# MLP products in another order: product 2 of group 0 ahead of product 1 of group 1, and three changes near the stage's ends

## The chip, the core and the metric

The kernel runs on one core of one Trainium2 chip. The metric is the device time of one execution in microseconds (us). TensorE (PE) multiplies; VectorE (DVE), ScalarE (ACT) and GpSimd (POOL) prepare its operands and take its results out of PSUM; SyncE (SP) issues most DMA transfers. In the traces each engine's instructions follow one another in the order of its own list, and they wait on semaphores for the other engines.

## The reference, cut to what matters

```python
def squared_relu_mlp(h, w1, w2):
    u = jax.nn.relu(h @ w1)
    return (u * u) @ w2

# for each of the 2 layers, x of 512 x 1024, all in float32:
#   x = x + mixer(rms_norm(x, norm_mix[layer]))     layer 0: attention, layer 1: a gated recurrence
#   x = x + squared_relu_mlp(rms_norm(x, norm_mlp[layer]), mlp_w1[layer], mlp_w2[layer])   # 1024 -> 4096 -> 1024
# return rms_norm(x, norm_final)
```

The change lies in the two MLPs and in the last normalization.

## The kernel before, in words

Every float32 product is made of three matmuls in a reduced format: each operand is split into a high half (a copy in that format, made on ACT) and a low half (the difference, made on DVE), and high by high, high by low and low by high are added up in PSUM. In the traces the halves of weights are called `wh` and `wl`; those of the hidden activations are `bh` and `bl` for group 0 and `sh` and `sl` for group 1.

The hidden width of 4096 is worked off in four quarters, `q4` = 0 to 3. A quarter has an up stage (activations times `w1`, squared ReLU into the tiles `u`) and a down stage (`u` times `w2`, added to the tokens' result `c`). Both use a Strassen-Winograd scheme: seven products P1 to P7 of sums of quarter blocks in place of eight. In the down stage each product is done for two groups, `g` = 0 and 1, one after the other into the same pair of PSUM banks, and 12 matmuls of 128x512 make one product of one group. The scheme has three running sums, each with its own two banks: X (`ps_t` in the down stage; P1, P6, P7 and P4 add to it in turn), V (`ps_acc`; P5 and P3) and W (`ps_z`; P2). After a product's group 1 the running sum is read by `collect`, which scales it and adds it to a part of `c` (`c<-ps_t,rr,c`, two DVE instructions, one for each bank). The next product of the same sum adds into the very banks that `collect` reads, so its first matmul waits for that read.

The order of a down stage's products stands in the table `ORDERS`: "mid" for all quarters but the last one of layer 1, which has "last". The list `steps` is run through once. Ahead of step `i` the loop calls `leave(i - 1)`, which first collects what step `i - 1` finished, if its group was 1, and then calls `prepare(i + 3)`: it makes the operand of the product three steps on. Operands come from the weight blocks b11, b12, b21 and b22. `added` sums two blocks in place for P5 and P6 (on DVE, `b<-b,b`; for P7, P4 and the first P6 by a DMA that accumulates, issued by POOL); `make` then splits the sum, `wh` on ACT and `wl` on DVE. What `prepare` also does, at places 20, 22 and 23 of the 28 places of a quarter, is to split one more piece of group 1's activations (`split_slot`, `sl<-u,sh`). Order on DVE and on ACT within the MLP is fixed: the class `Ordered` chains each instruction to the one recorded before it. So the order of calls in `leave` is the order in which DVE works.

In quarter 0, at places 19, 20, 24 and 25, `leave` also makes sums of blocks of the input `x` for the up stages (`sums_of_x`) and their halves (`halves_of_sums`, with the tiles `low`).

In layer 1 `end` takes over the last two steps, P4 of both groups: bank 0 of X holds tokens' part (2,0) and bank 1 part (3,0). It collects them, squares and sums the finished rows on ACT, takes the root, scales with `both`, `one` and `scaled`, and stores; all stores are issued by SP.

Of the kernel before, what the change touches and what calls it, by code (L numbers as in the profile page):

```python
# [18 lines left out]
S = 512  # L19
# [42 lines left out]
def hybrid_encoder(  # L62
# [23 lines left out]
    nc = tc.nc  # L86
    V, A, G, PE = nc.vector, nc.scalar, nc.gpsimd, nc.tensor
# [122 lines left out]
    behind = [None]  # L210
# [89 lines left out]
    with ExitStack() as actx:  # L300
# [12 lines left out]
        for i in range(2):  # L313
            both = []
# [460 lines left out]
    class Mlp:  # L775
# [299 lines left out]
        def collect(self, name, i, ps, cols=slice(0, S)):  # L1075
# [9 lines left out]


        ORDERS = {
            "mid": "P1 0 P5 0 P1 1 P2 0 P5 1 P6 0 P6 1 P3 0 P3 1 P7 0 P7 1 P2 1 P4 0 P4 1",
            "last": "P1 0 P5 0 P1 1 P2 0 P5 1 P2 1 P6 0 P6 1 P3 0 P3 1 P7 0 P7 1 P4 0 P4 1",
        }  # L1090

        def order(self, kind):
# [24 lines left out]
        def run(self, first, between, end):  # L1117
# [13 lines left out]
            def place(i):  # L1131

                return (i + self.STEPS // 2) % self.STEPS
# [21 lines left out]
            def make(i):  # L1155
                if i >= len(steps):
                    return
                name = steps[i][3]
                kind, q4, p, name = steps[i]
                at = 0  # L1160
                if kind == "up":
                    at = self.OPEN_AT if (p, name) == (0, "P1") else UP_AT
                ws[i] = made[i] = self.operand(self.source(unit(i), name), at)

                for before, x in (("P5", "P7"), ("P6", "P4")):
                    if name == before:
                        self.added(unit(i), x)

            def prepare(i):

                if i < len(steps) and steps[i][0] == "up":

                    if steps[i][3] == "P7" or self.layer and steps[i][1:] == (1, 0, "P4"):
                        return
                if i - 1 in range(len(steps)) and i - 1 not in made and i > 2:
                    make(i - 1)
                if i < len(steps) and steps[i][0] == "down":
                    add(i, 0)
                    if waiting and place(i) in (20, 22, 23):
                        self.split_slot(*waiting.pop(0))  # L1180
                make(i)
                for n in range(i + 1, i + 6):
                    add(n, n - i)

# [23 lines left out]
                elif at == 25 and q4 < NQ - 1:  # L1208
                    self.load(units["up", q4 + 1], (1, "b12"), (1, "b22"))

            def prepare_or_hold(i):

                if i + 1 < len(steps) and steps[i + 1][0] == "up" and steps[i + 1][3] == "P1":
                    held.append(i + 4)
                else:
                    prepare(i + 4)

            def leave(i):

                if i < 0:  # L1220
                    return
                kind, q4, p, name = steps[i]
                bank = sums[kind, q4, p if kind == "up" else 0][self.PRODUCTS[name][3]]
                if kind == "down":
                    if p:
                        for n in range(2):
                            self.collect(name, n, bank[n])
                    prepare_or_hold(i)
                    if q4 == 0:

                        k = {19: 2, 20: 2, 24: 3, 25: 3}.get(place(i))
                        if k:
                            (self.sums_of_x if place(i) in (19, 24) else self.halves_of_sums)(k)
                        if place(i) == 26:
                            self.replace()
                    return
                u, three = us[p], bank.rearrange("p (i n) -> p i n", i=2)
                keep = {"P1": 0, "P6": 1, "P5": 2, "P7": 3}.get(name)
                if keep is not None:

                    self.A.copy(u[keep], three)
                if held:
                    prepare(held.pop())
                    if p:
                        self.sums(0, slice(0, 2), slice(1, 4))
                at, x, y, op = {
                    "P3": (1, three, u[1], ALU.subtract),
                    "P7": (2, u[2], u[3], ALU.subtract),
                    "P2": (0, u[0], three, ALU.add),
                    "P4": (3, three, None, None),  # L1250
                }.get(name, (None,) * 4)
                if op:
                    self.V.tensor_tensor(u[at], x, y, op)
                if name == "P4":
                    self.A.activation(u[3], three, AF.Relu)
                    self.square(u[3])
                    if p:
                        last_sums(u, self.SUMS[:2])
                if later:
                    later.pop()()  # L1260
                prepare_or_hold(i)
                if op:
                    def rest(u=u, at=at):
                        self.A.activation(u[at], u[at], AF.Relu)
                        self.square(u[at])
                        if p:
                            self.split_slot(p, u[at], at)

                    if p and name == "P3":
                        later.append(rest)  # L1270
                    else:
                        rest()
                    if name == "P2" and not p:
                        self.split(p, slice(0, 2), slice(0, 3), slice(0, 3))
                elif name == "P4" and p:
                    last_sums(u, self.SUMS[2:3])
                    self.split_slot(p, u[2], 5)
                    last_sums(u, self.SUMS[3:])
                    waiting[:] = [(p, u[j], 3 + j) for j in (0, 1, 3)]
                elif name == "P4":  # L1280
                    self.sums(p, slice(0, 2), slice(1))
                elif name in ("P5", "P6") and p:
                    n = ("P5", "P6").index(name)
                    self.split(0, n, slice(0, 4), slice(3, 7))
# [63 lines left out]
    with ExitStack() as mctx:  # L1348
        mlp = Mlp(mctx, 0)
# [4 lines left out]
        last = {}  # L1354
# [57 lines left out]
    with ExitStack() as rctx:  # L1412
# [90 lines left out]
        def scaled(c):  # L1503
            OV.tensor_tensor(ps[f"c{c}"], ps[f"c{c}"], r, ALU.mult)
# [114 lines left out]
    with ExitStack() as mctx:  # L1619
# [57 lines left out]
            V.reciprocal(rt, rt)  # L1677
            return rt

        def store(t, h, cols=slice(0, S)):  # L1680
            nc.sync.dma_start(
                out=out[t * P : (t + 1) * P, h * S + cols.start : h * S + cols.stop],
                in_=mlp.y(t, h)[:, cols],
            )

        def both(t, h, rt, cols=slice(0, S), last=None):

            y = mlp.y(t, h)[:, cols]
            with tc.issue_after(last.ins) if last else nullcontext():
                V.scalar_tensor_tensor(y, y, rt, gb[h][:, cols], ALU.mult, ALU.mult)  # L1690
            store(t, h, cols)

        def one(t, h, rt, cols=slice(0, S), e=A, last=None):

            y = mlp.y(t, h)[:, cols]
            if e is A:
                with tc.issue_after(last.ins) if last else nullcontext():
                    A.activation(y, y, AF.Copy, scale=rt)
            else:
                V.tensor_scalar(y, y, rt, None, ALU.mult)  # L1700
            store(t, h, cols)

        def end(ws, xs):
            EG.turn(True)
            for t in range(2):
                square(t, 0, 0)
                scaled(t, 0)
                square(t, 1, 1, end=True)
                rt = root(t, 1)
                one(t, 0, rt)  # L1710
                both(t, 1, rt, last=mlp.gained)
            square(2, 1, 0)
            scaled(2, 1)
            square(3, 1, 0)
            scaled(3, 1, behind=mlp.y(1, 1))
            for g in range(2):
                mlp.times("P4", g, 0, ws[g], xs[0], False)
            mlp.collect("P4", 0, xs[0])
            square(2, 0, 1, end=True)
            two = root(2, 1)  # L1720
            mlp.collect("P4", 1, xs[1])
            parts = [slice(i * HS, (i + 1) * HS) for i in range(2)]
            for i, cols in enumerate(parts):
                ps = mlp.bank()[:, :HS]
                for g in range(2):
                    mlp.times("P4", g, 1, ws[g], ps, True, cols)
                mlp.collect("P4", 1, ps, cols)
                sq = square(3, 0, 1 + i, cols, end=i == 1)
                if i == 0:
                    both(2, 0, two)  # L1730
                    one(2, 1, two, last=sq)
                    scaled(3, 0, cols, behind=mlp.y(2, 0))
            rt = root(3, 2)
            both(3, 0, rt, parts[1])
            one(3, 1, rt)
            one(3, 0, rt, parts[0], V)

        end.ready = factors
# [70 lines left out]
```

## Time and profile before

| | us |
|---|---|
| median of 3 runs (1030.96 to 1031.72) | 1031.44 |
| the profiled execution | 1031.54 |
| its span, first to last instruction | 1029.5 |
| TensorE busy in the span | 1018.6 |
| VectorE busy | 857.8 |
| ScalarE busy | 700.9 |
| GpSimd busy | 172.6 |
| mean granted TensorE clock | 0.998 |

The profile of one execution gives each instruction's start and length, and for idle time the instruction whose end released it. `L765` is the helper of `Ordered`, so nearly all DVE and ACT instructions of the MLPs stand under that one line and are told apart by their tiles. The down stages' matmuls are line 1107, the up stages' 976, the last P4's 1070. A row that ends in x2 merges two instructions that follow each other.

### The profile page before, as it was taken

The page shows a single profiled execution, that of the slowest core. Times are in us where ns is not written, and L with a number is a line of the kernel's source. Part 1 is how long each engine was busy: PE and PEld are TensorE (multiplying, and loading weights), DVE is VectorE, ACT ScalarE, POOL GpSimd, SP SyncE. Part 2 cuts the span into 40 slices and gives each one's busy share as a digit, 9 for nine tenths or more (in the row PEclk, how much of TensorE's full clock was granted, in tenths as well). Part 3 has the DMA queues.
Part 4 walks back from the last instruction along what each step waited for, and adds up shares of the span by engine and source line. Part 5 has one row for each costly group of instructions (what it writes and reads, how often), then busy time and mean ns, then how long its engine had stood idle before and what let it go on. Part 6 is the DMA issues. An engine that isn't in the chain of part 4 may idle for free.

```text
span 1029.5 us, 15878 instructions
## 1 busy us (share of the span) xinstructions
PE 1018.6 (99%) x5862; PEld 892.2 (87%) x5862; DVE 857.8 (83%) x1148; ACT 700.9 (68%) x1083; POOL 172.6 (17%) x239
## 2 busy tenths in 40 slices
PE   8999999999999999999999999999999999999997
PEld 7888888888888988988988888888888988988986
DVE  6888787847789798898899888984689898898897
ACT  6777676835766873873875799964755774874865
POOL 0344344420010010010011121200010010010013
PEclk9999999999999999999999999999999999999999
DMA  7745454537537677667683575452436777677653
GB/s 236 216 124 144 105 153 103 155 110 265 156 81 197 169 156 194 174 146 199 177 209 80 156 184 151 103 220 86 97 71 182 169 159 196 168 149 200 174 109 111
DMA packets 53260, 160.46 MB, mean 156 GB/s; under 512 B 6720, under 2 KB 8256, under 8 KB 53184
## 3 DMA queue, kind: packets, MB, share of 16 engines
q1 hardware_dynamic: 42096, 120.35, 35.7%
q0 software_dynamic: 10656, 38.80, 23.1%
q8 instruction: 46, 0.75, 0.3%
q10 hardware_dynamic: 432, 0.31, 0.1%
q14 instruction: 30, 0.25, 0.1%
HBM read 137.41 MB, written 4.19 MB: 138 GB/s over the span
## 4 chain that ended last, share of the span: by engine, by line
PE 87%; DVE 6%; ACT 3%; issue 2%; DMA 1%; POOL 0%; SPq 0%; DVEq 0%; ACTq 0%; POOLq 0%
PE ps_t L1107 13%; PE ps_acc L1107 8%; PE ps_acc L976 7%; PE ps_z L976 5%; PE ps_acc L229 5%; PE ps_acc L231 5%; PE ps_acc L230 5%; PE ps_z L1107 4%; PE ps_o L976 3%; DVE wl L765 2%; PE ps_t L229 2%; PE ps_t L231 2%; PE ps_t L230 2%; PE ps_o L229 2%; PE ps_o L231 2%; PE ps_o L230 2%
## 5 line engine op out<-in xcount | busy, mean ns | idle before, releaser
L765 ACT CAST wh<-b 128x1024 fp32r<-128x1024 f32 x168 | 173.9, 1050 | 118.5 <-DVE b L765 73.5
L765 DVE TENSOR_TENSOR wl<-b,wh 128x1024 fp32r<-128x1024 f32 x168 | 202.9, 1219 | 38.9 <-ACT wh L765 37.6
L1052 POOL DMA_DIRECT2D b<-in_w_dn x40 | 35.0, 874 | 363.9 <-DVE b L765 268.4
L229 PE MATMUL ps_acc<-xgh,wh 128*128 128x512 f32 x192 | 78.5, 409 | 0.0
L231 PE MATMUL ps_acc<-xgl,wh 128*128 128x512 f32 x192 | 75.2, 392 | 0.0
L230 PE MATMUL ps_acc<-xgh,wl 128*128 128x512 f32 x192 | 75.1, 391 | 0.0
L224 DVE TENSOR_TENSOR wl<-raw,wh 128x512 fp32r<-128x512 f32 (+2 forms) x70 | 61.9, 912 | 14.2 <-ACT wh L222 14.1
L589 DVE TENSOR_TENSOR_SCAN scan<-keep,later 128x128 f32<-128x128 f32 (+1 forms) x64 | 59.5, 934 | 17.0 <-ACT keep L579 11.6
L765 ACT ACTIVATE u<-u 128x512 f32<-128x512 f32 x100 | 63.1, 633 | 11.3 <-DVE u L765 9.7
L222 ACT CAST wh<-raw 128x512 fp32r<-128x512 f32 (+2 forms) x70 | 50.6, 758 | 20.9 <-PE ps_acc L231 7.3
L593 POOL TENSOR_TENSOR w<-w,scan 128x128 f32<-128x128 f32 (+1 forms) x64 | 51.7, 809 | 57.2 <-DVE scan L589 54.0
L765 DVE TENSOR_TENSOR b<-b,b 128x1024 f32<-128x1024 f32 x48 | 58.7, 1223 | 1.3
L1052 POOL DMA_DIRECT2D b<-in_w_up x24 | 20.8, 868 | 231.1 <-DVE b L765 67.0
L765 DVE TENSOR_TENSOR u<-u 128x512 f32<-128x512 f32 (+1 forms) x92 | 54.9, 596 | 4.1 <-ACT u L765 2.1
L765 ACT CAST wh<-raw 128x1024 fp32r<-128x1024 f32 x46 | 48.1, 1047 | 2.5 <-PE ps_acc L1107 2.4
L1107 PE MATMUL ps_t<-wh,sl 128*128 128x512 f32 x120 | 47.0, 391 | 0.4 <-DVE sl L765 0.2
L1107 PE MATMUL ps_t<-wh,bh 128*128 128x512 f32 x120 | 46.8, 390 | 0.0
L1107 PE MATMUL ps_t<-wh,bl 128*128 128x512 f32 x120 | 46.8, 390 | 0.0
L1107 PE MATMUL ps_t<-wh,sh 128*128 128x512 f32 x120 | 46.7, 390 | 0.0
L765 DVE TENSOR_TENSOR sl<-u,sh 128x512 fp32r<-128x512 f32 (+2 forms) x50 | 37.4, 749 | 10.3 <-ACT sh L765 10.3
L976 PE MATMUL ps_acc<-low,wh 128*128 128x256 f32 x192 | 44.9, 277 | 0.5 <-DVE low L765 0.5
L765 DVE TENSOR_TENSOR wl<-raw,wh 128x1024 fp32r<-128x1024 f32 x36 | 44.3, 1229 | 0.8 <-ACT wh L765 0.8
(411 smaller groups left out, 3211.7 us busy)
## 6 DMA issues: line engine op xcount, KB each, us to landing
b<-in_w_dn SPq DMA_DIRECT2D x48, 512.0 KB, 4.4
b<-in_w_dn POOLq DMA_DIRECT2D x40, 512.0 KB, 5.8
b<-in_w_up SPq DMA_DIRECT2D x36, 512.0 KB, 4.8
b<-in_w_up POOLq DMA_DIRECT2D x24, 512.0 KB, 5.6
raw<-in_w_m SPq DMA_DIRECT2D x16, 512.0 KB, 4.5
raw<-in_w_dn SPq DMA_DIRECT2D x16, 512.0 KB, 4.6
raw<-in_w_in SPq DMA_DIRECT2D x16, 512.0 KB, 4.1
raw<-in_w_qk SPq DMA_DIRECT2D x12, 512.0 KB, 3.6
```

The costliest lines, as they stand in the source:

```text
L222: A.copy(wh[:, k, :], raw[:, k, :])
L224: V.tensor_tensor(wl[:, k, :], raw[:, k, :], f(wh[:, k, :]), ALU.subtract)
L229: PE.matmul(ps, wh, ah, start=start, stop=False)
L230: PE.matmul(ps, wl, ah, start=False, stop=False)
L231: PE.matmul(ps, wh, al, start=False, stop=stop)
L589: V.tensor_tensor_scan(sc[:, S - n : S][:, ::-1], keep[:, :n][:, ::-1], later[:, S - n :][:, ::-1], 1.0, ALU.mult, ALU.max,)
L593: G.tensor_tensor(wt, wt, sc[:, S - n + 1 : S + 1], ALU.mult)
L765: ins = getattr(self.e, name)(*args, **kwargs)
L976: PE.matmul(ps[:, i * HS : (i + 1) * HS], m, y, start=new and i == k == low == 0 and y is h, stop=(low, i, k) == steps[-1], skip_group_che ...
L1052: G.dma_start(out=unit[b].rearrange("p j n -> p (j n)"), in_=unit["src"](to), accum_op=ALU.add)
L1107: PE.matmul(sums[to][i], m, y[:, j, :], start=new and g == j == low == 0 and m is h, stop=g == low == j == 1, skip_group_check=not new,)
```

## The change

The order of products in a down stage is changed: P2 of group 0 is step 2 and P1 of group 1 is step 3, the other way round than before. In quarter 0, at place 25, the low halves of x's sums are made directly behind the operand, ahead of the additions of weights that `prepare` records last. In the end of layer 1 the running sum X is collected once more before P4, which then has a bank of its own for part (2,0) and is collected from it a second time; `both(2, 0)` moves behind the last half's collect; the store of part (3,1) is issued by ACT.

```diff
         ORDERS = {
-            "mid": "P1 0 P5 0 P1 1 P2 0 P5 1 P6 0 P6 1 P3 0 P3 1 P7 0 P7 1 P2 1 P4 0 P4 1",
-            "last": "P1 0 P5 0 P1 1 P2 0 P5 1 P2 1 P6 0 P6 1 P3 0 P3 1 P7 0 P7 1 P4 0 P4 1",
+            "mid": "P1 0 P5 0 P2 0 P1 1 P5 1 P6 0 P6 1 P3 0 P3 1 P7 0 P7 1 P2 1 P4 0 P4 1",
+            "last": "P1 0 P5 0 P2 0 P1 1 P5 1 P2 1 P6 0 P6 1 P3 0 P3 1 P7 0 P7 1 P4 0 P4 1",
         }
...
+            def prepare(i, then=None):
...
                 make(i)
+                if then:
+                    then()
                 for n in range(i + 1, i + 6):
                     add(n, n - i)
...
-                    prepare_or_hold(i)
+                    k = {19: 2, 20: 2, 24: 3, 25: 3}.get(place(i)) if q4 == 0 else None
+                    sums_or_halves = self.sums_of_x if place(i) in (19, 24) else self.halves_of_sums
+                    ahead = place(i) == 25 and k
+                    prepare_or_hold(i, (lambda: sums_or_halves(k)) if ahead else None)
                     if q4 == 0:
-                        k = {19: 2, 20: 2, 24: 3, 25: 3}.get(place(i))
-                        if k:
-                            (self.sums_of_x if place(i) in (19, 24) else self.halves_of_sums)(k)
+                        if k and not ahead:
+                            sums_or_halves(k)
...
         def end(ws, xs):
...
+            for i in range(2):
+                mlp.collect("P4", i, xs[i])
+            ps = mlp.bank()
             for g in range(2):
-                mlp.times("P4", g, 0, ws[g], xs[0], False)
-            mlp.collect("P4", 0, xs[0])
+                mlp.times("P4", g, 0, ws[g], ps, True)
+            mlp.collect("P4", 0, ps)
             square(2, 0, 1, end=True)
             two = root(2, 1)
-            mlp.collect("P4", 1, xs[1])
...
                 if i == 0:
-                    both(2, 0, two)
                     one(2, 1, two, last=sq)
-                    scaled(3, 0, cols, behind=mlp.y(2, 0))
+                    scaled(3, 0, cols, behind=mlp.y(3, 0)[:, cols])
+                else:
+                    both(2, 0, two, last=mlp.gained)
             rt = root(3, 2)
             both(3, 0, rt, parts[1])
-            one(3, 1, rt)
+            one(3, 1, rt, queue=A)
```

On DVE, at the start of quarter 2's down stage in layer 0, the instructions change places as follows (a minus is before, a plus is now). `wl<-raw` is the low half of P2's operand, `wl<-b_4740` that of P1 of group 1, `b_4740<-b_4740,b_4976` the addition for P5 of group 1, and `sl` and `u` are group 1's activations.

```order
 L765 TENSOR_TENSOR sl<-u,sh 128x2x256
 L765 TENSOR_TENSOR u<-u,ps_o 128x512
+L765 TENSOR_TENSOR wl<-raw,wh 128x1024
+L765 TENSOR_TENSOR sl<-u,sh 128x2x256
+L765 TENSOR_TENSOR u<-u 128x512 x2
 L765 TENSOR_TENSOR wl<-b_4740,wh 128x1024
 L765 TENSOR_TENSOR b_4740<-b_4740,b_4976 128x1024
-L765 TENSOR_TENSOR sl<-u,sh 128x2x256
-L765 TENSOR_TENSOR u<-u 128x512 x2
-L765 TENSOR_TENSOR wl<-raw,wh 128x1024
 L765 TENSOR_TENSOR u<-u 128x512
 L765 TENSOR_TENSOR sl<-u,sh 128x2x256
```

The low half of P1's operand and the addition behind it have moved behind the activations' instructions.

Some instructions further on DVE does the following. The first two rows are the low halves of P5 of group 1 and P6 of group 0; `b_4740<-b_4740,b_4980` is the addition for P6 of group 1, the third `wl` is the low half of that sum; `c_3131<-ps_t` is the collect of P1, `wl<-b_4978` the operand of P3, `c_3134<-ps_acc` the collect of P5.

```order
 L765 TENSOR_TENSOR wl<-b_4740,wh 128x1024
 L765 TENSOR_TENSOR wl<-b_4736,wh 128x1024
+L765 TENSOR_TENSOR b_4740<-b_4740,b_4980 128x1024
+L765 TENSOR_TENSOR sl<-u,sh 128x2x256
+L765 TENSOR_TENSOR wl<-b_4740,wh 128x1024
 L765 SCALAR_TENSOR_TENSOR c_3131<-ps_t,rr,c_3131 128x512 x2
-L765 TENSOR_TENSOR b_4740<-b_4740,b_4980 128x1024
-L765 TENSOR_TENSOR sl<-u,sh 128x2x256
-L765 TENSOR_TENSOR wl<-b_4740,wh 128x1024
 L765 TENSOR_TENSOR wl<-b_4978,wh 128x1024
 L765 SCALAR_TENSOR_TENSOR c_3134<-ps_acc,rr,c_3134 128x512 x2
```

The collect of P1 now stands behind the three instructions that make P6's operand of group 1; before, it stood ahead of them.

On DVE in quarter 0 of layer 1, near the end of the down stage, the three `low` rows are the low halves of x's sums and `b_7954<-b_7954,b_7958` is an addition of weights for the next up stage.

```order
 L765 SCALAR_TENSOR_TENSOR c_7345<-ps_z,rr,c_7345 128x512 x2
 L765 TENSOR_TENSOR wl<-b_7954,wh 128x1024
-L765 TENSOR_TENSOR b_7954<-b_7954,b_7958 128x1024
 L765 TENSOR_TENSOR low<-x,bl 128x256
 L765 TENSOR_TENSOR low<-x,s_7933 128x256
 L765 TENSOR_TENSOR low<-x,s_7352 128x512
+L765 TENSOR_TENSOR b_7954<-b_7954,b_7958 128x1024
 L765 TENSOR_TENSOR wl<-b_7954,wh 128x1024
 L765 SCALAR_TENSOR_TENSOR c_7347<-ps_t,rr,c_7347 128x512 x2
```

The addition has moved behind the three low halves.

## The prediction and its working

> **What bounds the kernel now.** I read the page first: how busy each engine is, and the clock.
>
> ```profile
> span 1029.5 us, 15878 instructions
> PE 1018.6 (99%) x5862; PEld 892.2 (87%) x5862; DVE 857.8 (83%) x1148; ACT 700.9 (68%) x1083; POOL 172.6 (17%) x239
> PEclk9999999999999999999999999999999999999999
> ```
>
> TensorE is busy for 1018.6 of 1029.5 us at nearly full clock. The change takes no matmul away, so all that it can win lies in the other 10.9 us, while every wait that it puts into TensorE's list lengthens the run by its own length. Next, TensorE's waits, longest first in total:
>
> ```profile
> PE ps_acc L435 <- ACT xgh L130: 1.7, 1, 1.7
> PE ps_z L391 <- DVE eps_t L119: 1.1, 1, 1.1
> PE ps_t L1070 <- DVE rt L1677: 0.5, 1, 0.5
> PE ps_acc L976 <- DVE low L765: 0.5, 1, 0.5
> PE ps_acc L435 <- ACT wh L201: 0.4, 1, 0.4
> PE ps_t L1107 <- DVE sl L765: 0.2, 1, 0.2
> ```
>
> Lines 391 and 435 are the kernel's start, which the change doesn't touch. The other three (last P4, x's low sums, P1 of group 1) sum to 1.2 us. With the slower restart behind each, and with a second wait of the last kind that shows in the next view, I put what these three edits can win at 2.2 us, and the store's at 0.3 us: 2.5 us together.
>
> Against that stands the state of VectorE where the order of products changes. The windows are the 12.7 us ahead of the first matmul of P6 of group 0, in the six down stages in which DVE does the collect of P1 with one product between it and P6 (quarters 1, 2, 3 of layer 0 and 0, 1, 2 of layer 1). Left out are quarter 0 of layer 0, where the first collect is a plain ACT instruction, and "last", where P2 of group 1 stands between as well. Columns: the window, its length, then busy PE, PEld, DVE, ACT, POOL.
>
> ```profile
> 368.50:381.20 12.70, 12.56 (x56) 10.07 (x55) 12.17 (x16) 8.09 (x12) 2.62 (x3) 1.00 0.77 159
> 445.00:457.70 12.70, 12.70 (x57) 10.49 (x56) 12.25 (x16) 8.02 (x12) 2.58 (x3) 1.00 0.76 160
> 521.40:534.10 12.70, 12.70 (x57) 10.51 (x56) 12.22 (x16) 8.15 (x12) 2.60 (x3) 1.00 0.84 192
> 753.60:766.30 12.70, 12.70 (x57) 10.52 (x57) 11.08 (x14) 6.41 (x7) 1.73 (x2) 1.00 0.35 69
> 831.90:844.60 12.70, 12.48 (x55) 10.03 (x54) 12.09 (x16) 8.17 (x12) 2.60 (x3) 1.00 0.78 160
> 908.50:921.20 12.70, 12.70 (x57) 10.49 (x56) 12.25 (x16) 8.01 (x12) 2.58 (x3) 1.00 0.78 158
> ```
>
> TensorE is short of 12.70 in the first and the fifth row alone, by 0.14 and 0.22 us: P1 of group 1, waiting for `sl`. DVE is busy for about 12.2 us of 12.7 in five of them and for 11.1 us in one. What is put ahead of something there delays it by its whole length.
>
> **The order of products.** I take quarter 2 of layer 0 for all six. First DVE's own rows:
>
> ```profile
> 446.40 1.22 DVE L765 TENSOR_TENSOR wl<-b,wh 128x1024 fp32r<-128x1024 f32 x1
> 447.66 1.23 DVE L765 TENSOR_TENSOR b<-b,b 128x1024 f32<-128x1024 f32 x1
> 448.80 0.68 DVE L765 TENSOR_TENSOR sl<-u,sh 128x512 fp32r<-128x512 f32 x1
> 449.67 1.42 DVE L765 TENSOR_TENSOR u<-u 128x512 f32<-128x512 f32 x2 [0.18 <-ACT u L765]
> 451.00 1.22 DVE L765 TENSOR_TENSOR wl<-raw,wh 128x1024 fp32r<-128x1024 f32 x1
> ...
> 453.94 2.35 DVE L765 TENSOR_TENSOR wl<-b,wh 128x1024 fp32r<-128x1024 f32 x2
> 456.22 1.40 DVE L765 SCALAR_TENSOR_TENSOR c<-ps_t,rr,c 128x512 f32<-128x512 f32 x2
> 457.54 1.21 DVE L765 TENSOR_TENSOR b<-b,b 128x1024 f32<-128x1024 f32 x1
> 458.67 0.68 DVE L765 TENSOR_TENSOR sl<-u,sh 128x512 fp32r<-128x512 f32 x1
> 459.92 2.36 DVE L765 TENSOR_TENSOR wl<-b,wh 128x1024 fp32r<-128x1024 f32 x2 [0.57 <-ACT wh L765]
> ```
>
> Then ACT's, which release some of them, and the first matmul of P6 on TensorE:
>
> ```profile
> 447.85 0.62 ACT L765 CAST sh<-u 128x512 fp32r<-128x512 f32 x1
> 449.00 0.63 ACT L765 ACTIVATE u<-u 128x512 f32<-128x512 f32 x1
> 457.70 0.39 PE L1107 MATMUL ps_t<-wh,bh 128*128 128x512 f32 x1
> ```
>
> Now: the collect of P1 starts at 456.22; its first half has ended by 456.96 (0.74 of the 1.40), and P6 starts 0.74 us later, as soon as TensorE gets to it.
>
> Step 1. P1's operand and the addition behind it move behind the activations. Today the addition (447.66) fills the time in which ACT finishes `sh` (448.47) and `u` (449.63). With P2's low half in the first place, DVE ends it at 447.62, waits for `sh` until 448.50, ends `sl` at 449.18 and waits for `u` until 449.67. From there all is as today, plus the addition: 1.25 us late. The cast for P5 waits for that addition, but P5 itself has room for it.
>
> Step 2. In the order of calls, the operand of P6 of group 1 comes ahead of the collect. What stands in the way is the addition at 457.54, the activations' half, and the low half that waits for ACT's cast of the sum; that low half ends 1.22 us behind 459.92, at 461.14. That is 3.6 us from 457.54, 3.5 net of the overlap between instructions. So the collect's first half ends at 456.96 + 1.25 + 3.5 = 461.7. On TensorE the collect's first bank is free only then, and P6 of group 0, which writes it, is next; behind it in TensorE's strict list stands everything else.
>
> Step 3. At the last P4, a matmul starts 0.15 us behind the collect that frees its bank (rows below: 1016.38 + 0.75 and 1017.28). So P6 starts at 461.85 in place of 457.70: 4.15 us, I take 4.1. Bounds of one such wait: 3.0, if DVE makes up step 1 (3.6 - 0.74 + 0.15); 4.3, if TensorE arrives earlier because P1's wait for `sl` is gone. Six of them: 24.6 us, between 18.0 and 25.8. P2's operand, which comes one step sooner, costs nothing: its `raw` is fetched long before, and its cast takes the place on ACT that P1's had. SP's and POOL's lists keep their order here. What P1 wins by its later place, in the fifth row's stage:
>
> ```profile
> 835.99 0.39 PE L1107 MATMUL ps_t<-wh,sh 128*128 128x512 f32 x1
> 836.94 0.40 PE L1107 MATMUL ps_t<-wh,sh 128*128 128x512 f32 x1
> ```
>
> These are its first and its third matmul, 0.95 us apart where two take 0.43 (16 in 3.41 us, below): 0.5 us, and about 0.4 in the first row's stage. It lies in front of the new wait and is swallowed by it.
>
> **The clock.** A wait of 4.1 us is longer than any that TensorE has now. What a long one does can be read at the kernel's start (clock in the third column from the end):
>
> ```profile
> 4.04:7.45 3.41, 1.31 (x6) 0.77 (x5) 2.02 (x6) 1.24 (x3) 0.00 (x0) 1.00 0.99 349
> 7.45:10.87 3.42, 3.42 (x9) 2.67 (x8) 2.51 (x5) 3.42 (x8) 0.00 (x0) 0.50 0.93 311
> 10.87:14.28 3.41, 3.41 (x16) 2.82 (x15) 3.41 (x7) 3.39 (x9) 0.00 (x0) 1.00 0.89 296
> ```
>
> In 3.41 us TensorE was busy for 1.31, so 2.1 us idle, and for the next 3.42 us the granted clock was 0.50, with 9 matmuls in place of 16. A wait of 4.1 us, wherever it lies in such stretches, leaves at least one of them with 2.05 us idle or more. A stretch at half clock costs up to 1.7 us; where part of it falls into the wait itself, less. Averaged over where the wait can begin I estimate 1.2 us for each, so 7.2 us for six, between 0 and 10.2.
>
> [...]
>
> **x's low sums, the last stage, the end.**
>
> ```profile
> 795.29 0.39 PE L976 MATMUL ps_acc<-low,wh 128*128 128x256 f32 x1 [0.46 <-DVE low L765]
> 1009.98 1.40 DVE L765 SCALAR_TENSOR_TENSOR c<-ps_t,rr,c 128x512 f32<-128x512 f32 x2
> 1011.20 0.39 PE L1107 MATMUL ps_t<-wh,bh 128*128 128x512 f32 x1
> 1016.38 0.75 DVE L765 SCALAR_TENSOR_TENSOR c<-ps_t,rr,c 128x512 f32<-128x512 f32 x1 [0.28 <-PE ps_t L1107]
> 1017.28 0.47 PE L1070 MATMUL ps_t<-wh,bh 128*128 128x512 f32 x1 [0.48 <-DVE rt L1677]
> 1023.32 0.48 DVE L765 SCALAR_TENSOR_TENSOR c<-ps_o,rr,c 128x256 f32<-128x256 f32 x1
> 1023.43 3.29 SPq L1681 DMA_DIRECT2D out<-c  x5
> ```
>
> The low sums' wait (0.46, some 0.7 with the restart) goes; it would go behind a longer wait earlier in that stage anyway. With a few stops of 0.1 us at P3 and P7 that also lie behind the new waits: 1.0 us won.
>
> In "last" P6 has another product's time, so no long wait there. But step 1's 1.25 us stay with DVE, and the collect ahead of P7 (first half ends 1010.73, matmul 1011.20, so 0.47 of room) comes 0.9 us too late, restart included. P4's bank of its own then takes 0.5 to 0.6 away (1017.28), while DVE has one collect of 0.74 more. The last collect (1023.32) follows `both` today and need not now, which just holds the rest of the delay; ACT's issue in place of one of SP's five (3.29 us) wins 0.3. I take 0 for the end, between -1 and +1.
>
> **The sum.** Against the profiled execution's own 1031.54 (the span and 2.0 us around it, 0.1 above the median of the runs): 1031.5 + 24.6 + 7.2 - 1.0 + 0 = 1062.3, so 1062.
>
> **The rivals.**
>
> 1. [...] Chance 0.23. [...]
> 2. The clock stays at half for a second stretch behind each wait: 6 x 1.7 = 10.2 more, 1072. Against it: the start has one such stretch only. Chance 0.06.
> 3. Not slower: the collect is not late, since DVE reaches it before TensorE comes to P6. That decides at 4.1 us of idle DVE in the 12.7 us ahead; the windows show 0.5 us, and 1.6 in one. Then the waits for `sl` (0.9 with restart), the low sums (0.7), P4's (0.6) and the store (0.3) are won: 1031.5 - 2.5 = 1029.0. Half of it would be lost in "last". Chance 0.06.
>
> **How the numbers follow.** The forecast has 0.65, and 1062 is its time. The range takes in the first rival and the low bound of the waits in part (1031.5 + 20 - 1 = 1050), and upwards 24.6 + 10.2 + 1 - 1 and part of the second rival (1070): 1050 to 1070. About 0.2% (2 us) can be told from no change here. Rivals 1 and 2 and the forecast are all slower: 0.94. The third is split: 0.03 faster by more than 0.2%, 0.03 within.
>
> **What would show it.** In the changed profile, TensorE's waits should have a row for `ps_t` at line 1107 on DVE's `c`, with six waits of about 4 us, each ahead of P6 of group 0, and the granted clock should show stretches of 0.5 behind them. DVE's busy time hardly changes (one collect more); its idle time grows. The wait of line 1107 on `sl` and that of `low` are gone. I am wrong if P6 starts without a wait, which would mean DVE had room that the windows don't show; or in size, if the waits are well under 3 us or the clock stays at 1.00.

## The result, and the profile after

The changed kernel takes 1065.64 us (median of 4 runs, 1065.35 to 1066.51) against 1031.58 for the kernel before on the same chip: a ratio of 1.0332, with a 95% interval from 1.0314 to 1.035. The forecast was 1062.0, with a range from 1050 to 1070. The profiled execution took 1065.61 us, 1063.8 of them span: 34.3 more than the span before.

First the head of the page.

```profile
span 1063.8 us, 15895 instructions
PE 1029.0 (97%) x5862; PEld 897.4 (84%) x5862; DVE 860.6 (81%) x1149; ACT 702.4 (66%) x1083; POOL 172.2 (16%) x239
```

Then TensorE's waits, longest in total first (us in total, times, longest).

```profile
PE ps_t L1107 <- DVE c L765: 24.9, 7, 4.2
PE ps_z L391 <- DVE eps_t L119: 1.1, 1, 1.1
PE ps_acc L435 <- ACT xgh L130: 1.1, 2, 0.9
PE ps_z L976 <- ACT u L765: 0.4, 1, 0.4
```

The row that heads the list was not there before: line 1107 waits for DVE's collect `c` seven times, 24.9 us in all. Six of the seven are P6 of group 0 in the six stages that the prediction named; the seventh is P7 in the last stage. The waits on `sl`, on `low` and ahead of the last P4 are gone. TensorE does the same 5862 matmuls in 1029.0 busy us in place of 1018.6, so there is a second loss in matmuls that run slower.

Next, quarter 2 of layer 0, DVE's rows that answer to those shown of before (6 to 11 us later in the span, some 6 of them from the stage ahead).

```profile
457.37 1.22 DVE L765 TENSOR_TENSOR wl<-b,wh 128x1024 fp32r<-128x1024 f32 x1
458.63 1.23 DVE L765 TENSOR_TENSOR b<-b,b 128x1024 f32<-128x1024 f32 x1
...
461.57 2.35 DVE L765 TENSOR_TENSOR wl<-b,wh 128x1024 fp32r<-128x1024 f32 x2
463.85 1.22 DVE L765 TENSOR_TENSOR b<-b,b 128x1024 f32<-128x1024 f32 x1
464.98 0.68 DVE L765 TENSOR_TENSOR sl<-u,sh 128x512 fp32r<-128x512 f32 x1
466.23 1.23 DVE L765 TENSOR_TENSOR wl<-b,wh 128x1024 fp32r<-128x1024 f32 x1 [0.57 <-ACT wh L765]
467.37 1.40 DVE L765 SCALAR_TENSOR_TENSOR c<-ps_t,rr,c 128x512 f32<-128x512 f32 x2
```

And TensorE's, from P5's last four matmuls to the first two of P6 of group 0.

```profile
463.13 1.07 PE L1107 MATMUL ps_acc<-wl,sh 128*128 128x512 f32 x4
468.26 0.60 PE L1107 MATMUL ps_t<-wh,bh 128*128 128x512 f32 x1 [4.06 <-DVE c L765]
468.67 0.63 PE L1107 MATMUL ps_t<-wh,bl 128*128 128x512 f32 x1
```

The addition, the low half of the activations and the operand of P6 of group 1 (463.85 to 467.46) now stand between the two low halves at 461.57 and the collect at 467.37. Its first half ends at 468.11, and P6 starts 0.15 behind that, at 468.26. P5's last four matmuls start at 463.13 and take 4 x 0.227, so TensorE is ready at 464.04: P6 is 4.22 us late. Counted in the same way the six waits are 4.36, 4.23, 4.21, 3.83, 4.35 and 4.22, together 25.2 us (the row above gives less, since it counts from the modelled end of a matmul; here and below I count by pitch, the distance from one matmul's start to the next, 0.227 us at full clock). The 3.83 belongs to the stage whose DVE had 1.6 us of idle time before and which has no `sl` to do.

The matmuls of P6 start 0.42 us apart and last 0.63. The windows of the clock show why. Below are the six stretches in which the granted clock (third column from the end) was 0.50, one for each wait.

```profile
386.53:389.94 3.41, 3.41 (x10) 2.67 (x9) 3.41 (x5) 0.93 (x2) 0.00 (x0) 0.50 0.99 150
468.45:471.86 3.41, 3.41 (x9) 2.63 (x9) 3.41 (x6) 0.68 (x2) 0.30 (x1) 0.50 0.86 136
550.37:553.78 3.41, 3.24 (x8) 2.59 (x9) 3.41 (x6) 1.04 (x2) 0.64 (x1) 0.50 0.90 139
789.30:792.71 3.41, 3.41 (x9) 2.64 (x8) 3.13 (x4) 1.37 (x2) 0.00 (x0) 0.50 0.98 150
871.22:874.63 3.41, 2.91 (x7) 2.36 (x8) 3.41 (x6) 1.37 (x2) 0.86 (x1) 0.50 0.90 142
953.14:956.55 3.41, 2.80 (x7) 2.27 (x8) 3.41 (x5) 1.48 (x3) 0.86 (x1) 0.50 0.97 159
```

At a clock of 0.50 I take half of a stretch's busy time as lost: (3.41 + 3.41 + 3.24 + 3.41 + 2.91 + 2.80) / 2 = 9.6 us. Set against the kernel before matmul by matmul, TensorE falls behind by 1.69, 1.69, 1.60, 1.70, 1.44 and 1.39 us more between P6's first matmul and the end of the slow ones, 9.5 together (there the matmuls are 0.427 us apart in place of 0.227). So 25.2 + 9.6 = 34.8 against the 34.3 us; the rest is a list of small items, below, that sum to -0.5.

### The profile page after: what moved, and what is told of

Read it like the earlier page. It is cut to its first block, busy times and chain, and to the rows that moved or that the text cites. A ratio compares the mean times of both kernels' runs of the same rounds, so it can differ in the third digit from the quotient of the medians.

```text
span 1063.8 us, 15895 instructions
## 1 busy us (share of the span) xinstructions
PE 1029.0 (97%) x5862; PEld 897.4 (84%) x5862; DVE 860.6 (81%) x1149; ACT 702.4 (66%) x1083; POOL 172.2 (16%) x239
## 4 chain that ended last, share of the span: by engine, by line
PE 78%; DVE 9%; ACT 6%; issue 5%; DMA 2%; SPq 0%; POOL 0%; DVEq 0%; ACTq 0%; POOLq 0%
PE ps_t L1107 13%; PE ps_acc L976 7%; PE ps_acc L1107 5%; PE ps_acc L231 5%; PE ps_acc L229 5%; PE ps_acc L230 5%; PE ps_z L976 4%; DVE wl L765 3%; PE ps_o L976 2%; PE ps_t L231 2%; PE ps_t L229 2%; PE ps_t L230 2%; DVE b L765 2%; PE ps_z L1107 2%; ACT u L765 2%
## 5 line engine op out<-in xcount | busy, mean ns | idle before, releaser
L1107 PE MATMUL ps_t<-wh,bh 128*128 128x512 f32 x120 | 52.1, 434 | 24.9 <-DVE c L765 24.9
L1107 PEld LDWEIGHTS ps_t<-wh,bh 128*128 128x128 f32 x120 | 25.0, 208 | 32.8 <-ACT sh L765 22.5
L1107 PE MATMUL ps_t<-wh,bl 128*128 128x512 f32 x120 | 51.3, 427 | 0.0
L765 DVE SCALAR_TENSOR_TENSOR c<-ps_t,rr,c 128x512 f32<-128x512 f32 (+1 forms) x59 | 41.3, 740 | 8.3 <-PE ps_t L1107 6.9
```

The costliest lines, as they stand in the source:

```text
L765: ins = getattr(self.e, name)(*args, **kwargs)
L1107: PE.matmul(sums[to][i], m, y[:, j, :], start=new and g == j == low == 0 and m is h, stop=g == low == j == 1, skip_group_check=not new,)
```

## The experiments

All times are medians beside runs of the kernel before on the same chip (1030.88 to 1031.20 us there).

**1. The order alone.** The kernel before with the two changed rows of `ORDERS` and nothing else.

```diff
-            "mid": "P1 0 P5 0 P1 1 P2 0 P5 1 P6 0 ...
+            "mid": "P1 0 P5 0 P2 0 P1 1 P5 1 P6 0 ...
```

> The kernel before with the two rows of the order alone. Theory (the whole loss sits in the order, the other edits win 1 to 2 us and part of that is swallowed): 1065.5 to 1067.5 us, with six waits of line 1107 on c of 3.8 to 4.4 us and one half-clock stretch of 3.41 us behind each. Rival (the last stage's or the low sums' edits cost time too): under 1064.5.

Measured: 1066.43 us, 1.0347 (1.0333 to 1.0361). The first row of TensorE's waits is that of the changed kernel to the digit:

```profile
PE ps_t L1107 <- DVE c L765: 24.9, 7, 4.2
```

The order makes the whole loss. The other three edits together are worth the 0.8 us between the two medians, or 1.5 us when each is set against its own runs of the kernel before, and that is not theirs alone: in one of the six stages of this run the half clock lasted for two stretches, which cost 1.6 us more (it is the run used for the clock, below).

**2. The order put back.** The changed kernel with the old two rows.

> The changed kernel with the order of products put back, so the low sums, the bank of the last P4 and the end's stores alone. Theory: 0.7 of the low sums' wait, 0.5 to 0.6 of the last P4's and 0.3 of the store are won: 1029.5 to 1030.5 us against 1031.5. Rival (the extra collect and the later gains at the end cost as much as they win): 1031 to 1032.5.

Measured: 1032.51 us, 1.0016 (1.0007 to 1.0025): slower by 1.6 us where I expected a gain. The expectation failed. To see which edit did it, the next two runs take them apart.

**3 and 4. The last stage alone; the low sums alone.** The first is the kernel before with the changed `end()`, `one()` and `store()`, the second the kernel before with the changed `prepare`, `prepare_or_hold` and `leave`.

```diff
+            for i in range(2):
+                mlp.collect("P4", i, xs[i])
+            ps = mlp.bank()
...
-                mlp.times("P4", g, 0, ws[g], xs[0], False)
+                mlp.times("P4", g, 0, ws[g], ps, True)
```

> The kernel before with the edits of the last stage alone: the last P4 in a bank of its own with one collect more, the later gains and the store on ACT. With the order put back, the stretch behind the last P4 took 0.73 us less than in the kernel before, and P7 had no wait ahead of it there. Theory (the last stage's edits win, the low sums' edit loses): 0.7 us under the kernel before, 0.1 to 1.2. Rival (the extra collect delays what follows): no gain, or up to 1 us more.

Measured: 1031.08 against 1031.20 us, 0.9997 (0.9988 to 1.0006). In the trace the stretch behind the last P4 is 0.73 us shorter up to the last matmul (650 ns of wait go), and from the last matmul to the end of the span it is 6.7 us in both, so the store's move shows nothing. The time does not resolve 0.7 us.

```diff
-                    prepare_or_hold(i)
+                    prepare_or_hold(i, (lambda: sums_or_halves(k)) if ahead else None)
```

> The kernel before with x's low sums ahead of the addition of weights, alone. Theory (from the trace with the order put back: the wait for low is gone, but the addition comes 2.6 us later, the cast of its sum on ACT with it, and the copy of u behind that cast, which TensorE then waits for: 1.26 in place of 0.62 us in layer 1, and 0.6 to 1.1 us in layer 0): 1.0 to 2.5 us over the kernel before. Rival (my prediction's 0.7 us won at the low sums): 0.5 to 1 us under it.

Measured: 1032.93 us, 1.0018 (1.0009 to 1.0027). Below, the rows of layer 1's quarter 0, first DVE and ACT in the kernel before.

```profile
791.29 1.22 DVE L765 TENSOR_TENSOR wl<-b,wh 128x1024 fp32r<-128x1024 f32 x1
792.54 1.23 DVE L765 TENSOR_TENSOR b<-b,b 128x1024 f32<-128x1024 f32 x1
793.85 1.05 ACT L765 CAST wh<-b 128x1024 fp32r<-128x1024 f32 x1 [2.93 <-DVE b L765]
```

Then DVE, ACT and TensorE in this run.

```profile
791.71 1.22 DVE L765 TENSOR_TENSOR wl<-b,wh 128x1024 fp32r<-128x1024 f32 x1
792.85 0.42 DVE L765 TENSOR_TENSOR low<-x,bl 128x256 fp32r<-128x256 f32 x1
793.18 1.22 DVE L765 TENSOR_TENSOR low<-x,s 128x256 fp32r<-128x256 f32 x2
794.31 1.22 DVE L765 TENSOR_TENSOR b<-b,b 128x1024 f32<-128x1024 f32 x1
...
795.62 1.05 ACT L765 CAST wh<-b 128x1024 fp32r<-128x1024 f32 x1 [4.28 <-DVE b L765]
796.57 1.13 ACT L765 CAST xgh<-s 128x512 fp32r<-128x512 f32 x2
797.61 0.57 ACT L765 COPY u<-ps_acc 128x512 f32<-128x512 f32 x1
...
798.24 0.38 PE L976 MATMUL ps_acc<-bh,wh 128*128 128x256 f32 x1 [1.09 <-ACT u L765]
```

The low sums come before the addition now, so TensorE no longer waits for them. But the addition, which started 1.25 us behind the low half ahead of it, now starts 2.60 behind it (794.31, from 791.71): 1.35 us later. (The 2.6 of my expectation took in the shift of the whole stage.) The cast on ACT waits for it, 4.28 us in place of 2.93, and behind that cast in ACT's list stands the copy that empties the bank of TensorE's next product. A stop of 0.62 us for DVE became one of 1.25 us for ACT (both by pitch; the row gives 1.09). In layer 0, where there was no wait to win, the same shift costs 0.87 us. This edit loses by itself.

**5 to 8. The collect at other places.** These four keep the changed order of products and move only the collect of P1 of group 1 on DVE: ahead of the addition (as in the kernel before), behind the addition, behind the addition and `sl`, and behind one low half more than in the changed kernel. The first edit in full; the others put the same two calls elsewhere in `prepare`, or behind it.

```diff
                 if kind == "down":
+                    if (name, p) == ("P2", 0):
+                        return
                     if p:
                         for n in range(2):
                             self.collect(name, n, bank[n])
+                    if (name, p) == ("P1", 1):
+                        prepare(i + 3)
```

> The changed kernel with its order of products, but the collect of P1 of group 1 goes ahead of the addition, the low half of the activations and the operand of P6 of group 1 on VectorE's list, as in the kernel before. Theory (step 2, the 3.5 us put ahead of the collect, makes the wait; step 1 leaves VectorE 1.25 us late): each of the six waits shrinks from 4.2 to 0.65 us, the clock holds, so 1031.5 + 6 x 0.65 - 1.5 = 1034 us, 1032.5 to 1036. Rival A (VectorE makes up step 1): no wait, 1029.5 to 1031. Rival B (what is late is the operand or P1 itself, not the collect's place): waits of 2 us and more stay, over 1045.

> As the one with the collect first, but the addition of P6's weights (1.21 us) stays ahead of the collect; the activations' low half and the operand follow it. Theory: six waits of 0.65 + 1.2 = 1.9 us, 11.3 us in all. In the changed kernel windows of 3.41 us with up to 1.5 us idle kept the full clock and those with 2.4 and more lost it, so 1.9 lies between. If the clock holds: 1031.5 + 11.3 - 1.5 = 1041 us. If each wait still brings a half-clock stretch, 1.2 to 1.6 us each: 1048 to 1051. Rival (the wait depends on something else than what stands ahead of the collect): as long as in the changed kernel, 1065.

> As the changed kernel, but the collect of P1 goes ahead of the operand of P6 of group 1 and behind the addition and the activations' low half. Theory for the waits: the 1.84 us measured with the addition alone ahead plus 0.6 to 0.7 for the low half, so 2.5 us in five stages and 1.4 in the one that has no low half there. Theory for the clock: in the runs so far windows with up to 1.9 us idle kept the full clock and those with 2.36 and more lost it, so a wait of 2.5 us brings a half-clock stretch only where almost all of it lies in one window of 3.41 us: in one to three of the five, 1.2 to 1.7 us each. 1043.8 + 5 x 0.65 = 1047 without, 1048.5 to 1052 with. Rival (any wait of over 2 us brings one): five stretches, 1054.

> As the changed kernel, but the collect of P1 goes also behind the low half of P3's operand, 1.15 us later still. Theory for the waits: 4.2 + 1.15 = 5.35 us, 6.9 us more in all. Theory for the clock: a wait of 5.35 covers a whole window of 3.41 us wherever it lies, and each wait brings one half-clock stretch, of which up to 1.9 us lie inside the wait: 5 to 9 us in place of 9.6, so 1068 to 1072. Rival (a window that begins with 0.7 to 1.9 us idle at half clock keeps the half clock, as once in the run of the order alone): second stretches in two or more of the six, 1073 to 1080.

Measured, in the order of the list above: 1041.38, 1043.76, 1048.62 and 1082.49 us. The row of TensorE's waits on the collect, one fence for each, in the same order:

```profile
PE ps_t L1107 <- DVE c L765: 3.6, 6, 0.7
```

```profile
PE ps_t L1107 <- DVE c L765: 10.6, 7, 1.8
```

```profile
PE ps_t L1107 <- DVE c L765: 13.5, 7, 2.4
```

```profile
PE ps_t L1107 <- DVE c L765: 31.1, 6, 5.3
```

In quarter 2 of layer 0, counted by pitch, P6 is late by 0.70, 1.84, 2.44, 4.22 (the changed kernel) and 5.37 us. The steps between them are 1.14, 0.60, 1.78 and 1.15: in the changed kernel's rows the addition takes 1.13 to the next start, `sl` 0.60, the operand with its wait for ACT the 1.79 from there to the collect (467.37), and the low half behind the collect 1.13. What stands ahead of the collect on DVE comes out of TensorE's time one for one; the 0.70 is step 1 of the prediction, which gave 1.25 + 0.15 - 0.74 = 0.66.

The waits came as expected in all four (with the collect first, 0.29 us in layer 1's quarter 0, whose DVE had idle time before); of the times only that behind `sl` did, 1048.6.

The collect first was expected at 1034 us and took 1041.4. Behind the wait of 0.70 each stage has further stops (0.08, 0.11, 0.28, 0.08), so that five stages lose 1.25 to 1.4 us, DVE's whole delay, and layer 1's quarter 0 loses 0.9. Together that is 7.5 in place of 3.9; P7's wait of 0.87 in the last stage, and the low sums, which lose here too (the wait for ACT's `u` of experiment 4 is in this run as well), make most of the rest.

Behind the addition, 1041 was expected with the clock held, and it took 1043.8. The 1.5 us that I took off for the other edits are not won, as experiments 2 to 4 show, and the four executions differ: the profiled one and one more have a mean clock of 0.999 and took 1042.8 and 1042.7, the other two have 0.997 and 0.995 and took 1044.7 and 1046.0. Where the clock of those two fell, no trace shows.

The late collect was expected at 1068 to 1072, with one half-clock stretch for each wait. That failed: at 1082.5 it lies above even the rival with second stretches (1073 to 1080), and second stretches are what its trace shows.

**The clock in these runs.** In the traces of the changed kernel, of the order alone and of these four I took TensorE's idle time, by pitch and without the stops of under 0.2 us, in each window of 3.41 us of the clock's record, and set it against the clock of the next window (of the windows at full clock, those with 0.94 us or more):

```
clock in the window   idle of 3.41 us        windows   clock in the next
1.00                  0.94 to 1.95           21        1.00 in all
1.00                  2.03 to 3.41           21        0.50 in all
0.50                  0 to 0.61              21        1.00 in all
0.50                  0.72 to 2.70           6         0.50 in all
```

The two windows at the ends of the gap between the first two rows (1.95 and 2.03), from the runs with the collect behind the addition and behind `sl`:

```profile
851.07:854.48 3.41, 1.63 (x8) 1.06 (x7) 3.41 (x5) 1.32 (x2) 0.86 (x1) 1.00 0.88 130
854.48:857.89 3.41, 3.41 (x17) 2.80 (x16) 3.41 (x5) 3.41 (x5) 0.86 (x1) 1.00 0.72 132
```

```profile
935.20:938.61 3.41, 1.38 (x6) 1.19 (x7) 3.41 (x5) 2.70 (x4) 0.75 (x1) 1.00 0.66 91
938.61:942.02 3.41, 3.41 (x10) 2.66 (x9) 3.41 (x6) 2.33 (x3) 0.86 (x1) 0.50 0.82 127
```

And windows of the last two rows, in the run of the order alone, where the half clock stayed for two windows:

```profile
865.87:869.28 3.41, 0.00 (x0) 0.00 (x0) 2.85 (x4) 2.39 (x3) 0.86 (x1) 1.00 0.67 103
869.28:872.69 3.41, 2.69 (x6) 2.15 (x7) 3.41 (x5) 1.59 (x3) 0.86 (x1) 0.50 0.94 144
872.69:876.11 3.42, 3.42 (x9) 2.64 (x8) 3.17 (x5) 1.04 (x1) 0.00 (x0) 0.50 0.96 270
876.11:879.52 3.41, 3.41 (x16) 2.81 (x15) 2.02 (x4) 1.05 (x1) 0.00 (x0) 1.00 0.83 252
```

In the profiled execution with waits of up to 1.95 us no window lost the clock (1042.84 us, clock 0.999). With waits of 2.5 us two of five did. With 5.0 to 5.5 us all six lost it, and in four of them the wait reached into the next window by 0.72 us or more, which then stayed at half. A seventh stretch, also double, followed a wait of 3.1 us ahead of P6 in the last stage, which the profile puts down to ACT's `sh`: five of seven were double, in a kernel of 1082.5 us. With every small stop counted the two gaps have other ends (2.03 and 2.12; 0.75 and 0.87), and no window changes sides. Both gaps are read off these runs; no kernel was made that puts a window into them.

**9. The wait filled.** If the half clock follows from TensorE's idle time alone, work of no use put into the wait must win its time back.

```diff
+                if self.pad and (low, i, j) == steps[-1]:
+                    for _ in range(self.pad):
+                        PE.matmul(sums[to][i], zero, wh[:, j, :],
+                                  start=False, stop=False, ...)
```

> The changed kernel with 18 matmuls of a zero weight tile put into P5 of group 1, ahead of its last matmul, in the six stages with a long wait. They add zeros to P5's bank (the output stays), take 18 x 0.227 = 4.09 us, and fill the wait that follows; the collect and all of VectorE's list stay as they are. Theory (the 9.6 us behind the six waits are the half clock, and TensorE's idle time brings it): P6 starts when it did, the waits are 0.3 us or less, no stretch at 0.50, and the time falls by 9.6 us, so 1056 us, 1055 to 1057.5. Rival (the slow matmuls behind the waits have another cause, or P5's later end delays VectorE's and ACT's lists): 1060 to 1066.

Measured: 1057.20 us (1056.83 to 1057.62), 8.4 us less than the changed kernel with 108 matmuls more (7.7 less, when each is set against its own runs of the kernel before). The head of its page, then its row of waits on the collect (the added lines move the numbers of lines by 8 and 2):

```profile
span 1055.1 us, 16111 instructions
PE 1044.8 (99%) x5970; PEld 912.4 (86%) x5970; DVE 861.4 (82%) x1150; ACT 703.2 (67%) x1083; POOL 173.6 (16%) x239
```

```profile
PE ps_t L1115 <- DVE c L767: 0.7, 1, 0.7
```

The only wait for the collect that is left is P7's, and there is no stretch at 0.50 between the kernel's start and its end. Of the 9.6 us expected 1.2 are missing. Set against the changed kernel's trace matmul by matmul, the six stretches give back 9.0 (a stop of 0.08 us behind P6's first matmul stays in five). In layer 1's quarter 0 the added matmuls take 0.2 us longer than the wait that they fill, and 0.2 are left of this profile's start, where one window ran at 0.50 and the changed kernel's had none. P6 still comes up to 0.3 us late, but it does so at the time at which it started in the changed kernel. So the loss parts into about 25 us in which P6 must wait, and 8 to 10 us of clock that the waiting brings.

No version beat the kernel before. The one that holds the only edits with a gain in the trace, those of the last stage, is the same as before within what the time resolves.

## Why the prediction was right, and where it was not

**The waits (24.6, between 18.0 and 25.8): 25.2.** Place, releaser and size came as forecast: six waits ahead of P6 of group 0, 3.83 to 4.36 us where I took 4.1. Both steps behind the number hold alone: step 2's instructions by the four places of the collect, step 1 by the 0.70 us that stay when the collect is back at its old place. DVE's idle time in the 12.7 us ahead (0.5 us, and 1.6 in one stage) had shown that there was nowhere to make this up.

**The clock (7.2, between 0 and 10.2): 9.6.** This is the term that was mis-sized, by 2.4 us. What I read off the kernel's start (2.1 us idle of 3.41, and the next window at 0.50) came again: in the table above all 21 windows with 2.03 us or more idle were followed by one at 0.50 and none of the 21 with 0.94 to 1.95 was, and in the changed kernel each wait of 3.83 to 4.36 us lost one window. The average over where a wait begins did not hold. I let a part of each half-clock stretch fall into the wait and came to 1.2 us each; in fact the stretch began between 0.61 us ahead of P6's start and 0.97 behind it, so nearly all of it fell on matmuls, 1.6 us each. The six are not six draws either: within a layer the stages recur after 82.0 to 82.3 us (once after 83.4), and from one half-clock stretch to the next within a layer it is 81.92 (386.53 to 468.45, 789.30 to 871.22), 24 windows, so a stage finds the windows almost where the stage ahead of it did (0.56, 0.19 and -0.17 us behind P6's start in layer 0).

Not all windows that lost the clock were empty: 10 of the 21 had 0.06 to 1.38 us of work in them (three of the six in the changed kernel among them; in the one from 785.89 to 789.30 TensorE was busy for 0.97 us).

**Rival 1 (the clock holds, 1031.5 + 24.6 - 1.0 = 1055.1)** is out, by the same windows: the clock held behind none of the six waits. With the waits filled and the clock held, the run took 1057.2. **Rival 2 (a second stretch, 1072)** did not occur in the changed kernel, and occurred once in the order alone; in these traces it came where a wait left 0.72 us or more (0.72 to 2.70, six windows) idle in a window that ran at 0.50. **Rival 3 (not slower)** is out.

**The low sums and small stops (-1.0): -0.1.** The wait for `low` went, as I said. I called that the whole effect, and did not ask who waits for the addition that is moved behind: ACT's cast, and the copy of `u` behind it. In the changed kernel layer 0 loses 1.05 us at the up products of quarter 1 (0.4 of them the `ps_z` row above). Layer 1 wins 0.75 at the low sums without the stop on ACT that experiment 4 has there; that the long wait ahead in the same stage gives DVE and ACT the time is my reading, and no run was made for it. P1's `sl` and small stops win 0.4. So of the 1.0 us that I took off 0.1 is left.

**The last stage and the end (0, between -1 and +1): +0.3.** P7 starts 0.86 us late (I gave 0.9), a little more is lost behind it (1.05 in all), and the last P4's stretch wins 0.73. The store's 0.3 was not seen.

**The rest.** By the first product behind the kernel's start the changed kernel's profile is ahead, and 0.7 us of that are left where the MLPs begin: in the kernel before one window there (7.45 to 10.87) ran at 0.50, in the changed one none. That is no effect of the change. These items (-0.1 + 0.3 - 0.7) sum to -0.5, and 34.3 - 25.2 - 9.6 = -0.5. Against the profiled execution the forecast was 3.3 us short: 2.4 from the clock, 0.6 from the waits, 0.9 from the low sums, 0.3 from the last stage, less the 0.7 of the start and 0.2 by which the time exceeds the span by less than before (1.8 in place of 2.0).

## What to carry to other kernels

When two products change places, look for the instruction that empties the bank of the moved one, and count what its list puts ahead of it now: on an engine with hardly any idle time, as DVE was here (0.5 us of 12.7 in five of the six stages), what stood ahead of the collect came out of TensorE's time one for one (steps of 1.14, 0.60, 1.78 and 1.15 us). The same count is due for the thing that a moved step is put in front of, whose own readers may stand ahead of something else on a third engine. A wait on TensorE is to be priced with its clock: in the profiled executions here windows with up to 1.95 us idle kept the clock at 1.00 behind them, and the six waits of 3.83 to 4.36 us cost 1.4 to 1.7 us each on top of their length.

## What the runs showed of the hardware

The granted clock was recorded in windows of 3.41 us, and in these six traces (the changed kernel, the order alone, the collect at four places) it went with TensorE's idle time in the window before. At full clock, windows with 0.94 to 1.95 us idle (stops of 0.2 us or more) were followed by 1.00, and those with 2.03 us or more by 0.50, 21 of each; at 0.50, those with up to 0.61 us idle were followed by 1.00 (21), and those with 0.72 us or more by 0.50 (6). Between those numbers nothing was measured. The place of a wait among the windows counted: in the run with the collect behind `sl`, five stages had waits of 2.43 to 2.54 us, and the two that lost the clock were those of which a single window held 2.03 us or more.
